# The RWKV chunk recurrence in 128x128 products, its inverse blocks joined in the batched solve

## The chip, the cores and the metric

One core of one Trainium2 chip runs the whole kernel. The metric is the device time of one execution in microseconds (us). The kernel before was run three times: 3341.92, 3346.59 and 3361.79 us, median 3346.59 us.

## The reference

One layer of a hybrid network over 512 latent tokens of width 2048 and 256 context tokens. One input projection feeds an mLSTM group and an RWKV-7 group of 16 heads (64 wide); both run forwards and backwards. An output projection and a gated convolutional FFN follow. The part that matters here is the RWKV scan, done per direction and head:

```python
def step(s, xs):
    r_t, w_t, k_t, v_t, kk_t, a_t = xs
    s = (s * w_t[:, :, None, :]
         - jnp.einsum("bhvk,bhk->bhv", s, kk_t)[..., None] * (kk_t * a_t)[:, :, None, :]
         + v_t[..., :, None] * k_t[..., None, :])
    return s, jnp.einsum("bhvk,bhk->bhv", s, r_t)
...
y_f, s_f = rwkv7_scan(..., state[2], False)
y_b, s_b = rwkv7_scan(..., state[3], True)
y = y_f + y_b
```

The latent scans start from the final state of the context scans.

## The kernel before

The dense products (input projections, output projection, FFN) hold nearly all the work of TensorE. Each takes a weight tile of 128x1024 floats that `wload` loads on SP's queue (L349) into one of 3 raw buffers (WRAW = 3); ScalarE rounds it to a high part (L299), VectorE takes the rest as a low part (L300), and TensorE makes three products of it (L370 to L372, L403 to L405 and their like).

The RWKV group works on 8 pairs of heads, two directions, and chunks of 64 tokens: 8 chunks of latent and 4 of context tokens for a pair and direction, 192 chunk steps in all. For a pair, `prep` makes the scaled keys and receivers of the chunks (KR, BK) and the products G between them, and stores these in a DRAM tile `GK_d` (L748 and L759 are two of the stores). `tsolve` inverts the 32x32 diagonal blocks of the chunks' triangular matrices for many chunks at once, one problem to a partition, on VectorE; it stores the blocks in DRAM (`ts_o`, L803, and back into `GK_d`, L808).

`chain_load` loads the operands of two chunks (`r_GK` L820 to L823, the values `r_UV` L825, an inverse block `t_XT` L830) and builds the off-diagonal block of the inverse with eight 32x32 products (L834, L838, through the PSUM tag `ct`). There are 96 such loads. `chain_step` then makes one chunk's products: the state against keys and receivers (L859, 128x128), two 64x64 products of G with the values (L861), two 64x64 products with the inverse (L865), the new state (L868, 128x128), and for latent tokens two 128x64 products for the output (L871). ScalarE copies results from PSUM to SBUF in between, VectorE updates the state `r_M`. The output is stored once for two chunks (L900), and `finalize_pair` loads it again (L921), normalises it and transposes it.

Every DMA named here is issued by SyncE (SP), on one queue, in order. The order of all instructions on every engine is fixed when the program is built, by a scheduler that runs a timeline simulation over the instructions (`schedule_with_timeline_sim=True`); weight loads are given a higher priority there (L343). So a weight load stands in SP's order somewhere between the loads and stores of the RWKV part.

Of the kernel before, what the change touches and what calls it, by code (L numbers as in the profile page):

```python
# [34 lines left out]
# column offsets inside w_in  # L35
# [4 lines left out]
# channel-major weight tiles  # L40
# [3 lines left out]
# columns of the per-channel vector pack  # L44
# [52 lines left out]
def body(tc, A, dbg=None):  # L97
# [28 lines left out]
    PB = {"acc": 2, "pre": 2, "ct": 1, "R": 3}  # L126
# [11 lines left out]
    # ---------------------------------------------------------------- constants  # L138
# [17 lines left out]
    gmask = cload("gmask", [P, 2, P])  # L156
# [11 lines left out]
    # the biases in a sigmoid, halved: sigmoid(x) = 1/2 + tanh(x / 2) / 2 shares its tables with Exp  # L168
# [6 lines left out]
    # ---------------------------------------------------------------- adaLN  # L175
# [12 lines left out]
    def ada_chunk(j, c0=0, n=512):  # L188
        """columns c0 to c0 + n of a chunk for both c"""
# [29 lines left out]
    def ada_late(j, after=None):  # L219
        """a chunk for c alone: DVE accumulates over the K tiles, the PE adds the partitions up"""  # L220
# [31 lines left out]
    def rsqrt_big(dst, src, scale, eps_ap, n):  # L252
# [3 lines left out]
        # one Newton step: y (1.5 - 0.5 x y^2)  # L256
# [45 lines left out]
    class HT:  # L302
        """hi/lo operand [128, 16 kt, n]"""
# [29 lines left out]
    # ---------------------------------------------------------------- weights  # L333
# [41 lines left out]
    def proj2(srcs, H):  # L375
        """two products side by side, for operands that are still coming in"""
# [14 lines left out]
    def proj_tm(t, H, evac):  # L391
        """token-major: [128 tok, 256 col] per token tile, two token tiles to a bank"""
# [16 lines left out]
    # ---------------------------------------------------------------- mLSTM  # L409
# [20 lines left out]
    def conv1d(pt, j, n, dst):  # L430
        """centred conv over tokens of PSUM pt -> dst"""
# [31 lines left out]
    def after_key(d, dst, lf, mi):  # L463
        """i and the decay after the key: exclusive suffix (fwd) / prefix (bwd) sums"""
# [5 lines left out]
    def to_tok(cols, srcs):  # L470
        """rows [64, 128] -> columns of tokb"""
# [19 lines left out]
    def gates_x():  # L491
        mi, lf, b2, mm = gates("x", NX)
        for d in range(2):
# [4 lines left out]
            for j in range(4):  # L498
# [9 lines left out]
                # i minus the sums, in the place of i  # L508
# [7 lines left out]
    def keep(pt, n, dst, fn=None):  # L516
        """a product's tile to DRAM"""
# [51 lines left out]
        # exponents, then the weights, in the score layout [key, query]  # L569
# [75 lines left out]
    # ---------------------------------------------------------------- RWKV  # L645
    lw = {}
    la = {}
    Mst = DT("Mst", [NPAIR, 2, P, P])
# [5 lines left out]
    def vproj(p, H, seg):  # L654
        """token-major v of two pairs, to DRAM"""
# [23 lines left out]
    def prep(p, s, seg, d=None):  # L679
        """operands of one direction's eight chunks of latent tokens, or of both directions' four of context"""  # L680
# [24 lines left out]
        BK = rp("r_BK", [P, 8, 128], 1)  # L705
# [26 lines left out]
        GK_d = DT("GK_d", [P, 2, 8, 256], 16)  # L732
        G_d = GK_d[:, 0].rearrange("p c (h t) -> p c h t", t=128)
        KB_d = GK_d[:, 1]
        sp.dma_start(KB_d[:, :, 0:kc], KR[:, :, 0:kc])
        # G^T[(b|k) s, (kappa|r) t] per chunk and head
        for hf in range(2):
            G = rp("r_Gp", [P, 4, 2, 128], GPB)
            gd = d if x else hf
            pgs = [PS("pre", [P, 4, 128]) for _ in range(2)]  # L740
            for c4 in range(4):
                for h, pg in enumerate(pgs):
                    hs = slice(64 * h, 64 * h + 64)
                    c = 4 * hf + c4
                    pe.matmul(pg[:, c4, 0:kc], BK[hs, c, :], KR[hs, c, 0:kc], start=True, stop=True)  # L745
            for h, pg in enumerate(pgs):
                dve.tensor_tensor(G[:, :, h, 0:kc], pg[:, :, 0:kc], gmask[:, gd, None, 0:kc].to_broadcast([P, 4, kc]), ALU.mult)
            sp.dma_start(G_d[:, 4 * hf:4 * hf + 4, :, 0:kc], G[:, :, :, 0:kc])  # L748
        # (b|k) e^(cum_C - cum), token-major, for the state
        for hf in range(2):  # L750
# [8 lines left out]
            sp.dma_start(KB_d[:, cs, kc:kc + 128], bt)  # L759
# [4 lines left out]
        for d in dirs:  # L764
            u = Unit()
            u.p, u.d, u.seg, u.nch, u.c0 = p, d, seg, nch, c0[d]
            u.GK_d, u.KB_d, u.G_d, u.gC, u.kd = GK_d, KB_d, G_d, gC, kd
# [3 lines left out]
    def tsolve(units):  # L771
        """(I - A^T)^-1 of the 32x32 diagonal blocks, a problem to a partition (backward: transposed)"""
# [7 lines left out]
        def blocks(u, b):  # L780
            """the unit's diagonal blocks in DRAM, and their partitions here"""
            bs = slice(32 * b, 32 * b + 32)
            q = u.p0 + b * u.q
            yield slice(q, q + u.q), u.G_d[bs, u.c0:u.c0 + u.nch, :, bs].rearrange("s c h t -> (c h) s t")

        for u in units:
            u.q, u.p0, u.so = 2 * u.nch, off[u.d], so
# [21 lines left out]

    def chain_load(u, tt):  # L810
        """operands of two chunks, and (I - A^T)^-1 put together from its blocks"""
        kc = 128 if u.seg == "x" else 64
        o = K()
        cu = u.c0 + 2 * tt
        GK = rk("r_GK", [P, 2, 2, 256], 6)
        o.G = GK[:, 0].rearrange("p c (h t) -> p c h t", t=128)
        o.KB = GK[:, 1]
        o.UV = rk("r_UV", [P, 2, 128], 6)
        if u.seg == "x":
            sp.dma_start(GK, u.GK_d[:, :, cu:cu + 2, :])  # L820
        else:
            sp.dma_start(o.G[:, :, :, 0:kc], u.G_d[:, cu:cu + 2, :, 0:kc])
            sp.dma_start(o.KB[:, :, 0:kc + 128], u.KB_d[:, cu:cu + 2, 0:kc + 128])  # L823
        po = (u.p % 2) * 128
        sp.dma_start(o.UV[64:128], v_d[u.seg][u.p // 2, tt, :, po:po + 128].rearrange("(b t) v -> t b v", b=2))  # L825
        fwd = u.d == 0
        fa, fb = (slice(0, 32), slice(32, 64)) if fwd else (slice(32, 64), slice(0, 32))
        XT = rk("t_XT", [64, 4, 32], 2)
        q = u.p0 + (0 if fwd else u.q) + 4 * tt
        sp.dma_start(XT[fa], u.so[1 if fwd else 0, q:q + 4].rearrange("a s t -> s a t"))  # L830
        pw = PS("ct", [64, 256])
        px = pw[:, 128:256]
        for i in range(4):
            pe.matmul(pw[fb, 32 * i:32 * i + 32], o.G[fa, i // 2, i % 2, fb], XT[fa, i, :], start=True, stop=True)  # L834
        ws = XT.rearrange("s a t -> s (a t)")
        act.copy(ws[fb], pw[fb, 0:128])
        for i in range(4):
# [634 lines left out]
```

## Time and profile before

| what | value |
|---|---|
| median of three runs | 3346.59 us |
| span of the profiled execution | 3344.3 us |
| PE (TensorE) busy | 3246.0 us, 97% |
| DVE (VectorE) busy | 2097.5 us, 63% |
| ACT (ScalarE) busy | 1197.9 us, 36% |
| POOL (GpSimd) busy | 51.0 us, 2% |

The page gives the profiled execution's time as its span; it agrees with the median to 2.3 us. Busy time of PE is the time during which a matmul was under way; a matmul of full-precision operands is two records in the trace. In a timeline row the first column is the start and the second the time to the end of the last instruction; matmuls overlap, so the distance from one start to the next, not the duration, is what a product costs TensorE. Rows of SPq are DMA issues on SyncE's queue; their duration is the time that the issue holds the queue, not the transfer. The RWKV part lies between about 244 and 1697 us of the span; before it is the conditioning, behind it the output projection's rest and the FFN.

### The profile page before, as it was taken

What the parts mean: (1) busy time and instruction counts of PE and PEld (TensorE: products, weight loads), DVE (VectorE), ACT (ScalarE), POOL (GpSimd) and SP (SyncE); (2) the same over time, 40 slices, a digit from 0 to 9 for tenths busy, and PEclk for the clock granted to TensorE, in tenths of its full rate; (3) what the DMA queues carried; (4) which work ended last, traced back from release to release, by engine and by line L of the source; (5) the groups of instructions that cost most, each with busy time, mean ns of one, the idle gap of its engine ahead of it and who ended that gap; (6) DMA issues with size and microseconds to landing.
All of it is one profiled execution on the core that took longest, in us unless ns stands there. A gap on an engine that the chain in (4) does not pass through costs nothing.

```text
span 3344.3 us, 50011 instructions
## 1 busy us (share of the span) xinstructions
PE 3246.0 (97%) x18566; PEld 2610.8 (78%) x18566; DVE 2097.5 (63%) x4010; ACT 1197.9 (36%) x2474; POOL 51.0 (2%) x113
## 2 busy tenths in 40 slices
PE   8999999999999999999998899999999999999998
PEld 5688778787787878777677688888888888888887
DVE  2578777777475776665754787465555555555657
ACT  4356544333334444344323432232222222222323
POOL 0000101000000000000000000000000000000000
PEclk9999999999999999999999999999999999999999
DMA  8878656566567678776764355333333333333332
GB/s 280 306 241 243 185 156 161 162 212 206 187 188 230 194 234 253 207 233 214 260 211 130 99 190 183 95 95 97 96 97 95 95 100 96 95 95 95 101 95 101
DMA packets 391938, 552.97 MB, mean 165 GB/s; under 512 B 131312, under 2 KB 256520, under 8 KB 391440
## 3 DMA queue, kind: packets, MB, share of 16 engines
q1 hardware_dynamic: 382048, 536.41, 51.9%
q10 hardware_dynamic: 9648, 13.37, 1.1%
q8 instruction: 147, 2.41, 0.3%
q14 instruction: 95, 0.78, 0.1%
HBM read 459.06 MB, written 90.61 MB: 164 GB/s over the span
## 4 chain that ended last, share of the span: by engine, by line
PE 82%; DMA 8%; DVE 6%; ACT 2%; issue 1%; SPq 1%; DVEq 0%; ACTq 0%
PE acc L372 12%; PE acc L371 12%; PE acc L370 12%; PE acc L1350 5%; PE acc L1351 5%; PE acc L1352 5%; DMA am<-in_wmod 3%; PE R L859 2%; PE R L861 2%; PE R L865 2%; PE pre L195 2%; PE acc L405 2%; PE acc L404 2%; PE pre L745 2%; PE acc L403 2%
## 5 line engine op out<-in xcount | busy, mean ns | idle before, releaser
L299 ACT CAST whi<-wraw 128x512 fp32r<-128x512 f32 (+1 forms) x948 | 569.7, 604 | 1319.8 <-PE acc L371 715.9
L300 DVE TENSOR_TENSOR wlo<-wraw,whi 128x512 fp32r<-128x512 f32 (+1 forms) x948 | 629.2, 666 | 457.5 <-ACT whi L299 440.6
L370 PE MATMUL acc<-H,whi 128*128 128x512 f32 x1920 | 761.7, 397 | 4.0 <-ACT ev L520 3.0
L372 PE MATMUL acc<-H,wlo 128*128 128x512 f32 x1920 | 761.4, 397 | 3.7 <-DVE wlo L300 3.7
L371 PE MATMUL acc<-H,whi 128*128 128x512 f32 x1920 | 761.1, 396 | 0.0
L372 PEld LDWEIGHTS acc<-H,wlo 128*128 128x128 f32 x1920 | 362.7, 189 | 83.8 <-DVE wlo L300 4.9
L370 PEld LDWEIGHTS acc<-H,whi 128*128 128x128 f32 x1920 | 362.9, 189 | 82.8 <-ACT ev L520 3.2
L371 PEld LDWEIGHTS acc<-H,whi 128*128 128x128 f32 x1920 | 362.8, 189 | 79.2 <-issue 3.6
L1354 DVE SCALAR_TENSOR_TENSOR x<-acc,mod,x 128x512 f32<-128x512 f32 (+1 forms) x192 | 135.6, 706 | 221.9 <-PE acc L1352 221.8
L1298 DVE SCALAR_TENSOR_TENSOR f_cv<-upad,fvec,f_cv 128x512 f32<-128x512 f32 x352 | 263.7, 749 | 7.2
L1350 PE MATMUL acc<-fh,whi 128*128 128x512 f32 x640 | 253.2, 396 | 0.0
L1351 PE MATMUL acc<-fl,whi 128*128 128x512 f32 x640 | 253.1, 396 | 0.0
L1352 PE MATMUL acc<-fh,wlo 128*128 128x512 f32 x640 | 253.1, 396 | 0.0
L232 DVE SCALAR_TENSOR_TENSOR adacc<-am,csil,adacc 128x512 f32<-128x512 f32 x240 | 179.4, 748 | 91.8 <-DMA am<-in_wmod 89.8
L404 PE MATMUL acc<-whi,H 128*128 128x256 f32 x512 | 155.7, 304 | 0.0
L403 PE MATMUL acc<-whi,H 128*128 128x256 f32 x512 | 154.6, 302 | 0.3 <-DVE ev L434 0.3
L405 PE MATMUL acc<-wlo,H 128*128 128x256 f32 x512 | 152.7, 299 | 0.3 <-DVE wlo L300 0.3
L1352 PEld LDWEIGHTS acc<-fh,wlo 128*128 128x128 f32 x640 | 120.2, 188 | 29.1
L1350 PEld LDWEIGHTS acc<-fh,whi 128*128 128x128 f32 x640 | 120.2, 188 | 29.0
L1351 PEld LDWEIGHTS acc<-fl,whi 128*128 128x128 f32 x640 | 120.2, 188 | 29.0
L876 DVE SCALAR_TENSOR_TENSOR r_M<-r_M,r_gC,R 64x64 f32<-64x64 f32 x352 | 98.3, 279 | 48.1 <-ACT r_yt L872 33.0
L1236 PE MATMUL acc<-H,whi 128*128 128x512 f32 x256 | 101.6, 401 | 9.0 <-ACT H L299 7.9
(346 smaller groups left out, 4837.3 us busy)
## 6 DMA issues: line engine op xcount, KB each, us to landing
am<-in_wmod SPq DMA_DIRECT2D x128, 512.0 KB
wraw<-in_wup SPq DMA_DIRECT2D x88, 512.0 KB
wraw<-in_wgate SPq DMA_DIRECT2D x88, 512.0 KB
wraw<-in_wdn SPq DMA_DIRECT2D x88, 512.0 KB
wraw<-in_wcm SPq DMA_DIRECT2D x72, 512.0 KB
r_GK<-GK_d SPq DMA_DIRECT2D x64, 512.0 KB
wraw<-in_wtm SPq DMA_DIRECT2D x56, 512.0 KB
GK_d<-r_Gp SPq DMA_DIRECT2D x32, 512.0 KB
```

What stands on the lines that cost most here:

```text
L299: act.copy(hi, t)
L300: dve.tensor_tensor(lo, t, hi.bitcast(F32), ALU.subtract)
L370: pe.matmul(pt[:, :n], hi(k8), H.h(k), start=k == 0, stop=False)
L371: pe.matmul(pt[:, :n], hi(k8), H.l(k), start=False, stop=False)
L372: pe.matmul(pt[:, :n], lo(k8), H.h(k), start=False, stop=k == KT - 1)
L403: pe.matmul(o, H.h(k)[:, xs], hi(k4), start=first, stop=False, skip_group_check=True)
L404: pe.matmul(o, H.l(k)[:, xs], hi(k4), start=False, stop=False, skip_group_check=True)
L405: pe.matmul(o, H.h(k)[:, xs], lo(k4), start=False, stop=k == KT - 1, skip_group_check=True)
L1298: dve.scalar_tensor_tensor(cv, u[:, a:a + GH, b:b + GW], fvec[:, f, tap:tap + 1], cv, ALU.mult, ALU.add)
L1350: pe.matmul(pt, hi(m)[:, k, :], th[:, cs], start=k == 0, stop=False)
L1351: pe.matmul(pt, hi(m)[:, k, :], tl[:, cs], start=False, stop=False)
L1352: pe.matmul(pt, lo(m)[:, k, :], th[:, cs], start=False, stop=k == GF - 1)
```

## The change

- `prep` stores stacked operands for each chunk in a DRAM tile `AB_d` [128, 8, 4, kc] and the triangular matrices in `T_d` [128, 8, 64]. Where it stored KR, G and the transposed BK in 1 + 2 + 2 DMAs for a unit of eight chunks, it now issues 3 + 12 + 6 (latent) or 2 + 8 + 6 (context).
- `tsolve` also joins the inverse blocks: for groups of two chunks, 128x128 block-diagonal operands N and W (zeroed on POOL, filled by DMA and by ScalarE copies), one product of 128x32 with N (L854) and one with W (L859) for each group; the result is copied to SBUF and stored back in `T_d` (L864). The eight 32x32 products in `chain_load` are gone, with the PSUM tag `ct`.
- `chain_v` loads state and values stacked: `r_UV` is [128, 2, 2, 2, 64], filled by four DMAs of 64 partitions (L881), each value block twice. It has 8 buffers.
- `chain_load` loads `r_GK` in one DMA (L890), and the inverse into the two diagonal halves of `r_T` (a memset on POOL and two DMAs, L894).
- `chain_step` makes three kinds of product, all 128x128 on TensorE: A (two for latent, one for context; L908 and L910), T (one; L917), B (two or one). The new state is written by VectorE straight into the next chunk's `r_UV`; the output is the sum of A's and B's halves (a VectorE addition per half), stored by two DMAs (L980).
- The PSUM tag `R` has 4 buffers instead of 3; `dynamic_dma_scratch_size=1024` is passed to the builder; comments are removed.

Over the program the products on TensorE (two records each) change by -2160 and +1024: 192 + 512 + 128 + 192 new ones are L854 and L859, L908, L910, L917. SP issues 3042 DMAs instead of 1754.

```diff
@@ prep
-        GK_d = DT("GK_d", [P, 2, 8, 256], 16)
...
-        sp.dma_start(KB_d[:, :, 0:kc], KR[:, :, 0:kc])
+        AB_d = DT("AB_d" if x else "ABc_d", [P, 8, 4, kc], 16 if x else 8)
+        T_d = DT("T_d", [P, 8, 64], 24)
...
+        sp.dma_start(AB_d[LO, :, 0, :], KR[LO, :, 0:kc])
+        if x:
+            for o, i in ((LO, HI), (HI, LO)):
+                sp.dma_start(AB_d[HI, :, 1, o], KR[HI, :, i])
...
-            sp.dma_start(G_d[:, 4 * hf:4 * hf + 4, :, 0:kc], G[:, :, :, 0:kc])
...
+            sp.dma_start(AB_d[HI, cs, 0, :], G[HI, :, 0, 0:kc])
+            sp.dma_start(AB_d[LO, cs, 1, :], G[LO, :, 1, 0:kc])
+            sp.dma_start(T_d[LO, cs, :], G[LO, :, 0, 0:64])
+            sp.dma_start(T_d[HI, cs, :], G[HI, :, 1, kc - 64:kc])
+            if x:
+                sp.dma_start(AB_d[:, cs, 2, HI], G[:, :, 0, HI])
+                sp.dma_start(AB_d[:, cs, 3, LO], G[:, :, 1, LO])
...
-            sp.dma_start(KB_d[:, cs, kc:kc + 128], bt)
+            sp.dma_start(AB_d[:, cs, 2, 0:64], bt[:, :, LO])
+            sp.dma_start(AB_d[HI, cs, 3, kc - 64:kc], bt[LO, :, HI])
+            sp.dma_start(AB_d[LO, cs, 3, kc - 64:kc], bt[HI, :, HI])
@@ tsolve
+        for k in range(0, len(units), 2):
...
+            pool.memset(N, 0.0)
+            pool.memset(W, 0.0)
...
+                        sp.dma_start(dst[64 * h:64 * h + 64, u.gs, :], src)
+                for i in range(4):
+                    sp.dma_start(N[32 * i:32 * i + 32, u.gs, 32 * i:32 * i + 32], beside(u, i))
...
+            for g in range(ng):
+                pe.matmul(pw[:, g, :], N[:, g, :], XT[:, g, :], start=True, stop=True)
+            for i in range(4):
+                r = slice(32 * i, 32 * i + 32)
+                act.copy(W[r, :, r], pw[r])
+            for g in range(ng):
+                pe.matmul(px[:, g, :], W[:, g, :], XB[:, g, :], start=True, stop=True)
+            O = rp("t_XT", [P, 8, 32], 1)[:, 0:ng]
+            dve.tensor_copy(O, px)
+            for u in us:
+                for i in range(4):
+                    sp.dma_start(beside(u, i), O[32 * i:32 * i + 32, u.gs, :])
@@ chain_v, chain_load
+    def chain_v(u, tt):
+        t = rk("r_UV", [P, 2, 2, 2, 64], 8)
+        po = (u.p % 2) * 128
+        for h in range(2):
+            v = v_d[u.seg][u.p // 2, tt, :, po + 64 * h:po + 64 * h + 64].rearrange("(b t) v -> t b v", b=2)
+            for k in range(2):
+                sp.dma_start(t[LOHI[1 - h], :, k, h, :], v)
+        return t
...
-        for i in range(4):
-            pe.matmul(pw[fb, 32 * i:32 * i + 32], o.G[fa, i // 2, i % 2, fb], XT[fa, i, :], start=True, stop=True)
...
+        o.AB = rk("r_GK", [P, 2, 4, kc], 6)
+        sp.dma_start(o.AB, u.AB_d[:, cu:cu + 2])
+        o.T = rk("r_T", [P, 2, 128], 6)
+        pool.memset(o.T, 0.0)
+        for hs in LOHI:
+            sp.dma_start(o.T[hs, :, hs], u.T_d[hs, cu:cu + 2, :])
@@ chain_step
-        pe.matmul(pR[0:kc], o.KB[:, ci, 0:kc], u.M, start=True, stop=False, skip_group_check=True)
-        for h, hs in enumerate(H2):
-            pe.matmul(pR[0:64, hs], o.G[64:128, ci, h, 0:64], UV[64:128, hs], start=False, stop=True, skip_group_check=True)
...
+        both(pA, o.AB[:, ci, 0:2], MV)
+        Rs = rk("r_Rs", [P, 64], 4)
+        for h, hs in enumerate(LOHI):
+            act.copy(Rs[hs], pA[hs, h])
+        pe.matmul(pU, o.T[:, ci, :], Rs, **f)
+        for h, hs in enumerate(LOHI):
+            act.copy(UV[hs, h], pU[hs])
+        both(pB, o.AB[:, ci, 2:4], UV)
...
+                    for h in range(2):
+                        sp.dma_start(u.y_d[at(u, i), :, 64 * h:64 * h + 64].rearrange("(b t) v -> t b v", b=2), o.y[LOHI[1 - h]])
```

SP's order, near the end of the RWKV part, where the first weight tiles of the output projection (`in_wout`) are loaded. Before:

```order
L228 DMA am_16687<-in_wmod 128x1024
L349 DMA wraw_17160<-in_wout 128x1024
L642 DMA hm_d_128<-r_r_16131 128x512
L1227 DMA ev_16763<-hm_d_128 128x512
L1227 DMA ev_16767<-hm_d_128 128x512
...
L593 DMA H_16861<-rows_d_130 128x256
L587 DMA H_16859<-rows_d_130 128x128
L593 DMA H_16859<-rows_d_130 128x128
L587 DMA H_16861<-rows_d_130 128x128
L575 DMA H_16862<-rows_d_130 128x512
L587 DMA H_16861<-rows_d_130 128x128
L349 DMA wraw_17199<-in_wout 128x1024
```

And in the change, the same place:

```order
L349 DMA wraw_18071<-in_wout 128x1024
L349 DMA wraw_18160<-in_wout 128x1024
L851 DMA t_X_12546<-T_d_12033 32x4x32 x4
...
L864 DMA T_d_10549<-t_XT_12536 128x1x32 x4
...
L894 DMA r_T_12893<-T_d_10549 64x2x64 x2
...
L881 DMA r_UV_13137<-v_x_136 64x2x64 x3
...
L980 DMA yr_d_12890<-r_yt_13529 64x2x64 x2
...
L565 DMA H_17860<-vc_d_115 128x2x256
L568 DMA H_17860<-in_nmask 128x256
L349 DMA wraw_18199<-in_wout 128x1024
```

Between two weight loads there were 28 DMAs; now there are 605 (412 rows of the order, many of them for several DMAs). Over the whole program before, no two neighbouring weight loads have more than 29 DMAs between them. In the change five stretches have more than 100, in their order 111, 121, 262, 254 and 605 DMAs (1353 in all; they follow weight loads 126, 140, 161, 180 and 190 of 482); the next longest has 68.

PE's order at the same place. Before, the small products stand between dense ones:

```order
L404 MATMUL acc_15514<-whi_15691,H_2688 128x256
L405 MATMUL acc_15514<-wlo_15692,H_2687 128x256
L865 MATMUL R_12415<-r_Rs_12419,r_GK_12289 64x64
L868 MATMUL R_12400<-r_UV_12273,r_GK_12272 128x128
L871 MATMUL R_12400<-r_UV_12273,r_GK_12272 64x64 x2
L865 MATMUL R_12415<-r_Rs_12419,r_GK_12289 64x64
L838 MATMUL ct_12457<-r_GK_12451,t_XT_12455 32x32 x4
L859 MATMUL R_12503<-r_M_2457_11995,r_GK_12434 128x128
L861 MATMUL R_12503<-r_UV_12435,r_GK_12434 64x64 x2
L403 MATMUL acc_15513<-whi_15695,H_2687 128x256
L404 MATMUL acc_15513<-whi_15695,H_2688 128x256
```

In the change there is a stretch of 300 rows with no dense product of a loaded weight, from this

```order
L370 MATMUL acc_17607<-H_2687,whi_17648 128x512
L371 MATMUL acc_17607<-H_2688,whi_17648 128x512
L372 MATMUL acc_17607<-H_2687,wlo_17649 128x512
L854 MATMUL pre_12514<-t_XT_12494,t_X_12492 128x32 x8
L859 MATMUL pre_12515<-t_XB_12495,t_Y_12493 128x32 x8
L854 MATMUL pre_12568<-t_XT_12548,t_X_12546 128x32 x8
L917 MATMUL R_12939<-r_Rs_12942,r_T_12893 128x64
...
L908 MATMUL R_14953<-r_UV_14663,r_GK_14833 128x64 x2
...
L640 MATMUL pre_16358<-c_ident_90,r_kd_16172 128x128
L1316 MATMUL acc_17915<-H_17759,whi_17918 128x512
```

where the last row is the next dense product (L1316, the output projection). Of the products in between, 376 are those of the chain and the join (248 of L908, 64 of L917, 64 of the join), 144 are other products of up to 128 columns, and 52 go over 257 or 512 columns. The other four stretches look alike and are shorter.

## Rows read from the trace of the kernel before

**Rows 1.** page parts 1 and 4: span; busy time by engine; chain by engine

```profile
span 3344.3 us, 50011 instructions
...
PE 3246.0 (97%) x18566; PEld 2610.8 (78%) x18566; DVE 2097.5 (63%) x4010; ACT 1197.9 (36%) x2474; POOL 51.0 (2%) x113
...
PE 82%; DMA 8%; DVE 6%; ACT 2%; issue 1%; SPq 1%; DVEq 0%; ACTq 0%
```

**Rows 2.** windows view, RWKV stretch: busy us of each engine, clock, DMA share, GB/s

```profile
244.00:1697.00 1453.00, 1410.01 (x9858) 1125.92 (x9857) 1000.72 (x2244) 611.40 (x1457) 48.15 (x90) 0.97 0.69 207
```

**Rows 3.** lines view, PE: the chain's products

```profile
L859 PE MATMUL R<-r_M,r_GK 128*128 128x128 f32 (+1 forms) x384 | 87.9, 311 | 3.4 <-DMA r_GK<-GK_d 2.2 <-DVE r_M L876 1.0
...
L865 PE MATMUL R<-r_Rs,r_GK 64*64 64x64 f32 x768 | 84.5, 232 | 2.8 <-DVE r_GK L839 2.4 <-ACT r_Rs L863 0.3
L868 PE MATMUL R<-r_UV,r_GK 128*128 128x128 f32 x352 | 76.9, 302 | 0.0
...
L871 PE MATMUL R<-r_UV,r_GK 128*64 128x64 f32 x512 | 58.5, 239 | 2.3 <-ACT r_UV L866 2.3
...
L834 PE MATMUL ct<-t_XT,r_GK 32*32 32x32 f32 x768 | 42.8, 194 | 1.0 <-DMA t_XT<-ts_o 0.9
```

**Rows 4.** timeline of PE about 1001 to 1009 us: start, time, engine, line, operation

```profile
1001.00 0.49 PE L859 MATMUL R<-r_M,r_GK 128*128 128x128 f32 x2
1001.42 0.44 PE L861 MATMUL R<-r_UV,r_GK 64*64 64x64 f32 x4
...
1004.91 0.43 PE L838 MATMUL ct<-r_GK,t_XT 32*32 32x32 f32 x8
1005.28 0.44 PE L865 MATMUL R<-r_Rs,r_GK 64*64 64x64 f32 x4
1005.65 0.39 PE L404 MATMUL acc<-whi,H 128*128 128x256 f32 x1
1005.87 0.28 PE L405 MATMUL acc<-wlo,H 128*128 128x256 f32 x1
...
1007.63 0.38 PE L859 MATMUL R<-r_M,r_GK 128*128 128x128 f32 x2
1007.85 0.39 PE L868 MATMUL R<-r_UV,r_GK 128*128 128x128 f32 x2
1008.17 0.45 PE L871 MATMUL R<-r_UV,r_GK 128*64 128x64 f32 x4
1008.54 0.44 PE L861 MATMUL R<-r_UV,r_GK 64*64 64x64 f32 x4
```

**Rows 5.** timeline of PE: first and last of 351 groups of products

```profile
306.96 0.28 PE L964 MATMUL acc<-whi,H 128*128 128x256 f32 x1
307.08 0.28 PE L965 MATMUL acc<-wlo,H 128*128 128x256 f32 x1
307.29 0.43 PE L859 MATMUL R<-r_M,r_GK 128*64 128x128 f32 x2
...
1616.57 0.44 PE L865 MATMUL R<-r_Rs,r_GK 64*64 64x64 f32 x4 [0.32 <-ACT r_Rs L863]
```

**Rows 6.** source views, SP issues: count, min/median/max ns, first and last start

```profile
L825 SPq DMA_DIRECT2D r_UV<-v_x x64: 579/611/1178, 698.8 to 1567.8; - x64
...
L900 SPq DMA_DIRECT2D yr_d<-r_yt x64: 319/544/1368, 880.0 to 1621.2; - x64
...
L349 SPq DMA_DIRECT2D wraw<-in_wup x88: 327/328/328, 1838.1 to 3201.2; - x88
...
L349 SPq DMA_DIRECT2D wraw<-in_wdn x88: 327/328/328, 2053.0 to 3281.4; - x88
```

**Rows 7.** timeline of SP: first, second, last of 35 issues in a dense stretch

```profile
469.01 0.49 SPq L803 DMA_DIRECT2D ts_o<-t_X  x1
469.55 0.48 SPq L808 DMA_DIRECT2D GK_d<-t_X  x1
...
490.43 0.63 SPq L823 DMA_DIRECT2D r_GK<-GK_d  x1
```

More of the change, by code (lines that the diff above doesn't have):

```diff
@@ new lines, in beside @@
+    def beside(u, i):
+        r = 64 * (i // 2) + u.fa
+        c = u.c0 + i % 2
+        return u.T_d[r:r + 32, c:c + u.nch - 1:2, u.fb:u.fb + 32]
+    LOHI = (slice(0, 64), slice(64, 128))
+    def chain_v(u, tt):
+        t = rk("r_UV", [P, 2, 2, 2, 64], 8)
+        po = (u.p % 2) * 128
+        for h in range(2):
+            v = v_d[u.seg][u.p // 2, tt, :, po + 64 * h:po + 64 * h + 64].rearrange("(b t) v -> t b v", b=2)
+            for k in range(2):
+                sp.dma_start(t[LOHI[1 - h], :, k, h, :], v)
+        return t
@@ L824, in chain_load @@
[L824 to L832, printed above, removed]
@@ L842, in chain_init @@
[L842 to L850 removed]
+        kc = 128 if u.seg == "x" else 64
+        o.AB = rk("r_GK", [P, 2, 4, kc], 6)
[4 more added lines that the diff above has]
+            sp.dma_start(o.T[hs, :, hs], u.T_d[hs, cu:cu + 2, :])
@@ L875, in chain_step, with both @@
-        for hs in H2:
-            dve.scalar_tensor_tensor(u.M[hs, hs], u.M[hs, hs], u.gC[hs, u.c0 + c:u.c0 + c + 1], pM[hs, hs], ALU.mult, ALU.add)
-        if last:
-            sp.dma_start(Mst[u.p, u.d], u.M)
+        MV, UV = o.V[:, ci, 0], o.V[:, ci, 1]
+        bank = PS("R", [P, 5, 64])
+        f = dict(start=True, stop=True, skip_group_check=True)
+        def both(out, w, rhs):
+            if x:
+                for h in range(2):
+                    pe.matmul(out[:, h, :], w[:, h, :], rhs[:, h, :], **f)
+            else:
+                pe.matmul(out.rearrange("p h v -> p (h v)"), w.rearrange("p h t -> p (h t)"), rhs.rearrange("p h v -> p (h v)"), **f)
@@ new lines, in chain_step @@
+        pA, pU, pB = bank[:, 0:2], bank[:, 2], bank[:, 3:5]
+        both(pA, o.AB[:, ci, 0:2], MV)
[6 more added lines that the diff above has]
+        both(pB, o.AB[:, ci, 2:4], UV)
+        if x:
+            for h in range(2):
+                hs = LOHI[1 - h]
+                act.copy(o.y[hs, ci, :], pA[hs, h])
@@ L880, in chain @@
+        if nxt is not None:
+            for h, hs in enumerate(LOHI):
+                dve.scalar_tensor_tensor(nxt(h), MV[hs, h], u.gC[hs, u.c0 + c:u.c0 + c + 1], pB[hs, h], ALU.mult, ALU.add)
+        if x:
+            for h in range(2):
+                hs = LOHI[1 - h]
+                dve.tensor_tensor(o.y[hs, ci, :], pB[hs, h], o.y[hs, ci, :], ALU.add)
     def chain(us, mid):
+        x = us[0].seg == "x"
+        n = us[0].nch // 2
+        at = lambda u, i: i if u.d == 0 else n - 1 - i
@@ L882, in chain @@
+        nV = []
         for u in us:
-            chain_init(u)
-        n = us[0].nch // 2
+            V = chain_v(u, at(u, 0))
+            nV.append(V)
+            for h, hs in enumerate(LOHI):
+                m = V[hs, 0 if u.d == 0 else 1, 0, h]
+                if x:
+                    sp.dma_start(m, Mst[u.p, u.d, hs])
+                else:
+                    pool.memset(m, 0.0)
+            if x:
+                u.y_d = DT("yr_d", [4, P, 128], 16)
         for i in range(n):
-            if us[0].seg == "x" and i == 1:
+            if x and i == 1:
@@ L902, in chain @@
+            if x:
+                for u, o in zip(us, ops):
+                    for h in range(2):
+                        sp.dma_start(u.y_d[at(u, i), :, 64 * h:64 * h + 64].rearrange("(b t) v -> t b v", b=2), o.y[LOHI[1 - h]])
+        if x:
             mid()
@@ L1440, in pack @@
     o["selg"] = (idx[:, None] % 32 == np.arange(2)[None]).astype(f)
-    gm = np.zeros((P, 2, P), f)
+    gm = np.zeros((P, 2, 2, P), f)
     s_ = (idx % 64)[:, None]
     t_ = (idx % 64)[None]
-    strict = idx[None] < 64
-    gm[:, 0] = np.where(strict, s_ < t_, s_ <= t_)
-    gm[:, 1] = np.where(strict, s_ > t_, s_ >= t_)
+    for h in range(2):
+        strict = (idx[None] // 64) == h
+        half = np.where(((idx[:, None] // 64) != h) & ~strict, f(0.5), f(1))
+        gm[:, 0, h] = np.where(strict, s_ < t_, s_ <= t_) * half
+        gm[:, 1, h] = np.where(strict, s_ > t_, s_ >= t_) * half
     o["gmask"] = gm
```

131 lines of the change are left out of this document (61 added, 70 removed).

## Prediction

> **What bounds the kernel now.** I read the page first: PE is busy for 3246.0 us of the 3344.3 us span, and 82% of the chain that ended last is PE's own work [rows 1]. The windows view of the RWKV stretch says the same there: PE is busy for 1410 of 1453 us, while DVE has 450 us free, ACT 840 us, POOL nearly all, and the DMA engines are busy for 0.69 of the time at 207 GB/s [rows 2]. So the sum of PE's slots sets the time, and whatever lies on another engine is hidden, as long as the next weight tile is there when PE asks for it. The views that follow are PE's lines and its timeline, for what the chain's products cost; then SP's issues by line and its timeline, because the order shown above moves SP more than anything else.
>
> **PE: what is removed.** The lines view gives counts in records, two to a product [rows 3]; the slots come from the timeline, from one start to the next [rows 4].
> - L859, a 128x128 product ahead of two 64x64 ones: 1001.42 - 1001.00 = 0.42 us, 192 times: 81 us.
> - L865, two 64x64: 1005.65 - 1005.28 = 0.37 us, 192 times: 71 us; its twin L861 the same: 71 us.
> - L834, four 32x32, and its twin L838 (1005.28 - 1004.91 = 0.37 us): 96 times each: 71 us.
> - L868: 1008.17 - 1007.85 = 0.32 us, 176 times: 56 us. L871: 1008.54 - 1008.17 = 0.37 us, 128 times: 47 us.
>
> That is 397 us. They stand in 351 groups between dense products, and going into one costs PE something as well: L965 ahead of such a group takes 307.29 - 307.08 = 0.21 us where the same product before it takes 0.12 [rows 5], and the first dense product behind a group takes 1005.87 - 1005.65 = 0.22 us [rows 4]. With 0.09 and 0.10 us that is 0.19 x 351 = 67 us (first group at 307.29, last at 1616.57). In all 464 us.
>
> **PE: what is added.** 1024 products of the 128x128 kind. L859 at 1007.63, with L868 of the same shape behind it, has a slot of 0.22 us [rows 4]; the 0.42 at 1001.00 holds the step to the 64x64 tile behind it. Nothing changes shape any more, so I take 0.22: 225 us. The upper end is 0.42, a rival below. PE's path becomes 3344.3 - 464 + 225 = **3105 us**, if nothing else stops PE.
>
> **DVE, ACT and POOL.** 256 more additions on DVE, 504 more copies on ACT and 144 more memsets on POOL stand beside hundreds of free us on each [rows 2]; I cost them at nothing. If that cover were gone they would show as waits of L908 or L917. The DMA engines carry some 18 MB more; at 207 GB/s for a share of 0.69 that is 60 us of engine time against 0.31 x 1453 = 450 us free, nothing too.
>
> **SP: what the change does to the queue.** SP gets 1288 more DMAs. This isn't spread evenly. Before, a weight load has at most 29 other DMAs between it and the next. In the new order there are five stretches without a weight load, of 111, 121, 262, 254 and 605 DMAs, 1353 in all. The queue is in order: the next dense tile can't start to load until all of them are issued. In these stretches PE's order holds only small work, and behind it dense products that wait for the tile.
>
> *What the 1353 issues take.* 464 of them load 64 partitions in pieces; the row of that kind is the old r_UV load, median 0.611 us. 327 store 64 partitions; the nearest row is L900, 0.544 us. The other 562 I take at the price of a plain weight load, 0.328 us [rows 6]. This sums to 646 us. Between issues lies 469.55 - 469.01 - 0.49 = 0.05 us [rows 7], 68 us more: 714 us, or 0.53 each. The other view is the densest stretch of the old queue, much of it the same kind of loads and stores of pieces: 35 issues from 469.01 to the last one's end at 491.06, or 0.63 each [rows 7], which would be 852 us. I take the middle, 0.58: **785 us**. The ends far apart are 0.328 for each issue without a gap (444 us) and 0.63 (852 us); 0.58 is nearer the second because nearly three in five of these issues are of the dear kinds.
>
> *What PE has to do meanwhile.* In the longest stretch 376 products of 0.22 us (83 us), and 144 small and 52 wider ones, which I estimate at 42 us by their columns: 125 us. The other four, counted alike, give 15, 16, 35 and 34 us: 225 us together. And three weight tiles may be there ahead, one for each raw buffer. The FFN's loads give the price of a tile: 264 of them (the up, gate and down rows, 88 each) lie between 1838.1 and 3281.4 us [rows 6], 5.5 us of PE each, so up to 16 us a stretch, 81 us in all. Cover: 306 us.
>
> *Exposed:* 785 - 306 = 479 us, in which PE stands still although it would have dense work. Waits for semaphores on SP come on top; I cost them at nothing here, and as a rival below.
>
> **The sum.** 3105 + 479 = 3584 us against the profiled execution, whose span is 2 us under the median of 3346.59: **3586 us**, 7% slower. At 0.53 us an issue it is 3518, at 0.63 us 3653; this case's own range, with 30 us for the cover, is 3490 to 3690. The saving of 239 us is undone where the five stretches expose as much: (306 + 239) / 1353 = 0.403 us an issue is the point that decides.
>
> **A rule to weigh.** The rows of one kind of issue range from 0.328 to 0.611 us [rows 6], so the price follows what is moved. [...]
>
> **The rivals.**
> - *Faster: SP keeps up.* If pieces of 64 partitions cost the queue no more than a plain load when nothing else crowds the DMA engines, all issues go at 0.328 us, without a gap or with one of 0.05: 444 to 511 us, 138 to 205 exposed, 3245 to 3312 us. It decides below 0.403 us an issue. For it: L900 has been issued in 0.319 us at its best, and the rows of before were taken while the DMA engines were busy for 0.69 of the time. Against it: the old r_UV load never took less than 0.579 us in 64 issues [rows 6]. Chance 0.16.
> - *No change.* A mean issue between 0.38 and 0.43 us balances the saving: 3313 to 3380 us. It needs no more than that the dear kinds cost 0.46 instead of 0.544 to 0.611 us at 0.328 for the rest [rows 6]; against it the medians by themselves give 0.48. Chance 0.11. [...]
> - *Slower still: the queue stops.* SP's stretches hold stores of results that the chain has yet to make (T_d from L864, yr_d from L980) and loads into buffers that it has yet to free. A store that waits at the head of the queue holds the loads behind it, which the chain needs next; PE's small work would then follow the issues instead of lying beside them. If all 225 us of it loses its place: 3811 us; half, 3700. For it: work and queue depend on each other in every chunk. Against it: 8 buffers of r_UV and 6 of r_GK and r_T let loads run ahead. Chance 0.14.
> - *The products stay dear.* If a 128x128 product keeps a slot of 0.42 us, the new ones cost 430 us and the saving is 34; outside of the stretches, where SP hides them, at most 205 us come on top: up to 3791 us. The slot at 1007.63 speaks against it. Chance 0.04.
>
> **How the numbers follow.** My forecast has 0.55: 3586 us. A difference under 1% (33 us) can't be told from no change here. The range, 3300 to 3790 us, takes in the forecast's own, no change, the upper end of the faster case and most of the third and fourth; it leaves out some 0.13 below and 0.06 above. Faster by over 1%: 0.16; within 1%: 0.11; slower: 0.73.
>
> **What would show it.** In the new profile PE idles in five stretches, ended by a weight tile (wraw, through L299 or L300), the longest by far at the start of the output projection, where L1316's first product waits for some 200 us; SP's timeline there shows issues with hardly a gap between them. The lines view gives L908 and L917 slots of 0.22 us and no product with 32 or 64 rows in the chain; behind the RWKV part the rows are as before. I am wrong if PE stays busy through these stretches (SP faster than 0.40 us an issue, or the tiles there earlier than the order says), or if PE's idle time is ended by r_T, r_UV or yr_d instead, which is the third rival.

## The result: 17% slower, and 350 us beyond the forecast

The change takes 3935.75 us (median of 4 runs, 3934.54 to 3936.90) against 3351.36 us for the kernel before in the same comparison: a ratio of 1.174, 95% interval 1.171 to 1.177. The sign was forecast (3586 us); the size lies outside the range of 3300 to 3790 us.

The page of the change, its span, its busy times, PE's share by slice, and the engines of the chain that ended last:

```profile
span 3935.1 us, 48383 instructions
...
PE 3293.6 (84%) x16294; PEld 2722.0 (69%) x16294; DVE 2130.6 (54%) x4186; ACT 1318.0 (33%) x2989; POOL 98.6 (3%) x257
...
PE   8997999676975984674375589999999999999998
...
PEclk9999999686975975655567799999999999999999
...
PE 60%; DMA 15%; SPq 10%; DVE 7%; ACT 4%; issue 3%; POOL 0%; DVEq 0%; ACTq 0%; POOLq 0%
```

PE has 2272 matmul records fewer than before [rows 1] and yet is busy 48 us longer, while the granted clock falls in the slices where PE idles (to 5 tenths in the twentieth, where PE is busy for 3 tenths). With each 2 us of busy time counted at the clock granted in it, PE is busy for 3017 us against 3199 before, 182 us less. DMAs and SP's queue, 9% of the chain of before [rows 1], now hold 25% of it. Windows of the change (us of each engine, granted clock, DMA share, GB/s): 200 us out of the longest stretch without a weight load, and the dense end.

```profile
1700.00:1900.00 200.00, 91.03 (x396) 78.02 (x394) 107.95 (x262) 59.90 (x186) 8.66 (x19) 0.53 0.64 174
2300.00:3800.00 1500.00, 1478.41 (x6452) 1207.75 (x6452) 876.65 (x1312) 438.39 (x712) 0.00 (x0) 0.99 0.34 112
```

No engine and not the DMA engines (0.64, before 0.69 [rows 2]) are full in the first of them. The prices of the new issues on SP (count, min/median/max ns, first and last start):

```profile
L881 SPq DMA_DIRECT2D r_UV<-v_x x256: 573/605/1686, 889.7 to 2010.0; - x128
...
L894 SPq DMA_DIRECT2D r_T<-T_d x192: 573/602/1710, 461.9 to 2026.3; - x192
...
L980 SPq DMA_DIRECT2D yr_d<-r_yt x128: 574/580/1615, 1097.0 to 2047.5; - x128
```

They are as dear as the nearest rows of before said [rows 6]: 0.58 to 0.605 us at the median. Added up over the five stretches without a weight load, the 1353 issues hold the queue for 775 us, 0.573 each. But the stretches last 1033 us: 67, 85, 187, 184 and 508 us from the end of one weight load's issue to the next (the last from 1636 to 2145). What PE waits for longest in this profile (us, times, longest):

```profile
PE pre L854 <- DMA t_X<-T_d: 110.4, 13, 50.5
PE pre L773 <- DVE r_Gp L758: 46.3, 16, 5.9
PE R L908 <- issue: 41.5, 6, 10.0
PE pre L854 <- DMA t_XT<-ts_o: 40.1, 6, 12.3
PE acc L1316 <- ACT H L299: 37.6, 7, 15.3
PE R L908 <- DMA r_GK<-AB_d: 34.9, 16, 9.5
...
PE acc L370 <- ACT whi L299: 14.4, 5, 9.6
```

A weight tile (a wait for `whi` or `wlo`) is far from the head of the list. The waits that it ended add up to 31 us of 627; those ahead of the chain's products (L908, L910, L917) make 180 us, of the join's (L854, L859) 159 and of prep's 87. The output projection (L1316) waits for H, its other operand, which is made from the results of the heads. In the longest stretch its first product started at 2063 us, 82 us before the next weight tile was issued:

```profile
2063.01 1.22 PE L1316 MATMUL acc<-H,whi 128*128 128x512 f32 x2 [15.26 <-ACT H L299]
```

Of SP's own waits over the whole program, the longest behind the weight loads' wait for a free buffer, and one of the chain's:

```profile
SPq L228 <- DVE adacc L232: 76.2, 57, 3.0
SPq L228 <- DMA am<-in_wmod: 74.5, 36, 6.0
...
SPq L980 <- DVE r_yt L931: 27.3, 29, 5.3
```

L228 loads the weights of the conditioning, which have nothing to do with the chain; L980 stores the chain's output. The longest single wait of PE stands at the join: its product with N waits for blocks that went through DRAM. One solve and join in SP's timeline and then in PE's, both of the change:

```profile
1896.30 3.33 SPq L829 DMA_DIRECT2D T_d<-t_X  x4
1899.68 2.32 SPq L829 DMA_DIRECT2D T_d<-t_Y  x4
1902.04 1.29 SPq L849 DMA_DIRECT2D t_XT<-ts_o  x2
1903.37 1.27 SPq L849 DMA_DIRECT2D t_XB<-ts_o  x2
1904.74 2.50 SPq L851 DMA_DIRECT2D t_X<-T_d  x4
1907.28 1.27 SPq L849 DMA_DIRECT2D t_XT<-ts_o  x2
1908.59 1.28 SPq L849 DMA_DIRECT2D t_XB<-ts_o  x2
1909.91 2.54 SPq L851 DMA_DIRECT2D t_X<-T_d  x4
```

```profile
1914.05 1.89 PE L854 MATMUL pre<-t_XT,t_X 128*128 128x32 f32 x8 [3.36 <-DMA t_X<-T_d]
1917.68 3.59 PE L859 MATMUL pre<-t_XB,t_Y 128*128 128x32 f32 x16 [1.74 <-POOL t_X L837]
1933.33 3.59 PE L854 MATMUL pre<-t_XT,t_X 128*128 128x32 f32 x16 [12.06 <-DMA t_XT<-ts_o]
1936.75 0.66 PE L917 MATMUL R<-r_Rs,r_T 128*128 128x64 f32 x2
1938.10 0.66 PE L917 MATMUL R<-r_Rs,r_T 128*128 128x64 f32 x2 [0.69 <-DMA r_T<-T_d]
```

Stores (L829), loads that read them (L851), the products with N (L854), copies into W, the products with W (L859), stores of the result (L864); then the same for the next two units. Each waits for the one before, each DMA stands in one queue at 0.6 us, and the T products of the chain (L917) wait for the blocks that the join stores. From 1794 to 1936 us no chunk step gets its T product. From the first output store of one group of 32 latent steps (two pairs of heads, both directions) to that of the third after it, it is 880 to 1475 us before (L900), 198 us a group, and 1097 to 1953 us now (L980), 285 us a group.

### The profile page after: what moved, and what is told of

It is laid out like the page before. It is cut to its first block, busy times and chain, and to the rows that moved or that the text cites. A ratio compares the mean times of both kernels' runs of the same rounds, so it can differ in the third digit from the quotient of the medians.

```text
span 3935.1 us, 48383 instructions
## 1 busy us (share of the span) xinstructions
PE 3293.6 (84%) x16294; PEld 2722.0 (69%) x16294; DVE 2130.6 (54%) x4186; ACT 1318.0 (33%) x2989; POOL 98.6 (3%) x257
## 2 busy tenths in 40 slices
DMA packets 582535, 571.43 MB, mean 145 GB/s; under 512 B 379248, under 2 KB 455176, under 8 KB 582032
## 4 chain that ended last, share of the span: by engine, by line
PE 60%; DMA 15%; SPq 10%; DVE 7%; ACT 4%; issue 3%; POOL 0%; DVEq 0%; ACTq 0%; POOLq 0%
PE acc L370 10%; PE acc L372 10%; PE acc L371 9%; PE acc L1430 4%; PE acc L1432 4%; PE acc L1431 4%; DMA am<-in_wmod 4%; PE R L908 2%; SPq L829 2%; PE pre L195 1%; DVE adacc L232 1%; DMA r_GK<-AB_d 1%; PE acc L1316 1%; PE acc L1317 1%; PE acc L1318 1%
## 5 line engine op out<-in xcount | busy, mean ns | idle before, releaser
L908 PE MATMUL R<-r_UV,r_GK 128*128 128x64 f32 x1024 | 209.4, 369 | 131.0 <-issue 41.5
L908 PEld LDWEIGHTS R<-r_UV,r_GK 128*128 128x128 f32 x1024 | 196.6, 280 | 161.4 <-issue 63.1
L854 PE MATMUL pre<-t_XT,t_X 128*128 128x32 f32 x192 | 37.1, 343 | 152.2 <-DMA t_X<-T_d 110.4
L405 PE MATMUL acc<-wlo,H 128*128 128x256 f32 x512 | 152.5, 301 | 4.9 <-DVE wlo L300 4.9
L404 PE MATMUL acc<-whi,H 128*128 128x256 f32 x512 | 153.4, 300 | 0.0
L1316 PE MATMUL acc<-H,whi 128*128 128x512 f32 x256 | 104.1, 412 | 55.9 <-ACT H L299 37.6
L927 DVE SCALAR_TENSOR_TENSOR r_UV<-r_UV,r_gC,R 64x64 f32<-64x64 f32 x320 | 89.0, 278 | 109.4 <-ACT r_yt L924 84.3
```

Of the source, the lines that this page charges most:

```text
L404: pe.matmul(o, H.l(k)[:, xs], hi(k4), start=False, stop=False, skip_group_check=True)
L908: pe.matmul(out[:, h, :], w[:, h, :], rhs[:, h, :], **f)
```

## The experiments

All ratios are to the kernel before, run on the same chip (medians 3348 to 3351 us). The expectations name their theories by letters. Q: SP's in-order queue sets the time once it is full. P: each issue costs the same, full queue or not. S: the number of SP's issues sets the time, whatever they are for. J: the path through solve and join, where each step waits for the one before. C: the new chain waits for its own results, or PE's clock falls. K: the fallen clock makes the stretch long.

**More issues, old products.** In the kernel before, `chain_load` got 13, in another run 6, loads that nobody reads:

```diff
+        for i in range(13):        # the other run: 6
+            sp.dma_start(rk("dmy", [P, 2, 128], 2)[64:128], v_d[...].rearrange("(b t) v -> t b v", b=2))
```

> The kernel before with 13 more loads in every chain_load (1248 loads of 64 partitions from v_d into a scratch tile that nobody reads), so SP issues 3002 DMAs as the change does, and PE's products are those of before. Theory Q (SP's in-order queue, some 0.6 us for each issue, sets the time): its order has stretches of 172 and 633 DMAs without a weight load; 805 x 0.65 = 523 us less about 300 us of PE work and tiles at hand, so 3450 to 3700 us. Rival C (the change is slow because the new chain waits for its own results or because PE's clock falls): no such chain here, 3340 to 3390 us.

> As the run with 13 more loads, but 6 in every chain_load: 576 more issues, 2330 in all on SP. Its order has one stretch without a weight load, of 122 DMAs, and by the last tile of the input projections 160 of 192 chunk steps are placed (the kernel before: 166; the one with 13 loads: 128). Theory Q (SP's queue decides once it is full, and the chain then falls behind the dense work and is left standing alone at the end): SP has room for these, 3345 to 3450 us. Rival P (each issue costs the same, full queue or not; 636 us for 1248): 3630 to 3660 us.

Measured: 3987.56 us (1.191, 1.188 to 1.194) and 3519.75 us (1.050, 1.046 to 1.054). So 576 loads cost 169 us, 0.29 each, and the next 672 cost 468, 0.70 each. Added loads on SP alone can make the kernel before slower than the change is, with none of the new products. The price of one added issue, in SP's rows of the run with 13, and what SP waits for ahead of these issues:

```profile
L827 SPq DMA_DIRECT2D dmy<-v_x x832: 573/577/2397, 1020.5 to 2411.6; - x167
```

```profile
SPq L827 <- DMA dmy<-v_x: 322.7, 404, 3.7
SPq L827 <- DMA dmy<-v_c: 137.9, 177, 4.0
```

The added loads share two scratch buffers, and SP stands still until a buffer's last load has landed: 461 us in this run, 256 us in the one with 6. So the two prices hold the waits for these buffers as well as the issues; a queue that fills up would give the same picture, but these runs don't show it by itself.

Both runs came out above the upper end that the theory of a full queue (Q) gave them; the same price for each added load whatever the queue holds (P, 3630 to 3660 us for the run with 6) is refuted by the low price of the first 576.

**Other queues.** The change with DMAs moved from SP (`sp.dma_start` becomes `act.dma_start` or `pool.dma_start`): prep's stores and the join to ScalarE and the chain's loads to GpSimd; all of these to GpSimd; prep's stores and the join to ScalarE alone (there with the lead of the weight loads lowered to 300 as well).

> The change with the DMAs of prep's AB_d and T_d stores and of the join issued by ScalarE, and the loads of chain_v and chain_load issued by GpSimd; SP is back at 1522 DMAs, the products are the same. Theory Q: PE's path of 3105 us plus what the one stretch left (360 DMAs, some 75 us exposed) costs: 3150 to 3300 us. Rival C (chain's own waits, PE's clock): the chain and its order are nearly the same, so 3700 to 3940 us. If ScalarE's or GpSimd's issues hold up the chain: between, 3300 to 3600 us.

> The change with all of these DMAs (prep's AB_d and T_d stores, the join, chain_v and chain_load) issued by GpSimd, 1520 there and 1522 on SP. Theory Q: as long as GpSimd issues one in under 0.8 us, 3150 to 3300 us; at 1 us or more its own queue becomes the bound, 3400 us or above. Rival C: 3700 to 3940 us.

> The change with prep's AB_d and T_d stores and the join's DMAs issued by ScalarE (848 of them), the chain's loads staying on SP (2194 issues), and the lead of the weight loads lowered to 300. Theory S: 2194 issues, fewer than the 2330 that cost the kernel before 169 us: 3250 to 3500 us. Theory J: 3650 to 3800 us.

Measured: 3826.68 us (1.143, 1.140 to 1.145), 4167.77 us (1.244, 1.241 to 1.247) and 3854.42 us (1.150, 1.148 to 1.152). Halving SP's issues gave back 109 us, where theory Q gave 636 or more. An issue costs ScalarE and GpSimd what it costs SP, as one row each of the first and the second run shows (SP's medians for the two lines are 0.575 and 0.605 us), and the path through the join is as long as it was: PE's longest wait in the first run is still the same one.

```profile
L864 ACTq DMA_DIRECT2D T_d<-t_XT x128: 309/582/1467, 426.5 to 1852.0; - x128
```

```profile
L881 POOL DMA_DIRECT2D r_UV<-v_x x256: 585/599/644, 1025.8 to 2279.8; - x128
```

```profile
PE pre L854 <- DMA t_X<-T_d: 105.5, 9, 43.3
```

So occupation of SP's queue alone is not the cause: theories Q and S failed in all three, and J, with 3650 to 3800 us for the last, came nearest, though still under it; rival C's 3700 to 3940 us holds for the first run and not for the second.

**Another order.** Only the scheduler's lead of the weight loads: `AHEAD_X = 3000` becomes 12000, or 2000.

> The change with the scheduler's lead of the weight loads raised from 3000 to 12000: the stretches of 111 to 262 DMAs go, and the last one grows from 605 to 1187. Theory Q: the same number of issues, but the cover is less at the end: 1187 x 0.62 = 736 us against some 250 us of PE work in it, and what was exposed before is saved; 3600 to 3900 us. Rival C: no change, 3900 to 3950 us.

> The change with the scheduler's lead of the weight loads lowered from 3000 to 2000: the same 3042 issues on SP, but by the last tile of the input projections 160 steps are placed instead of 107, the last stretch without a weight load has 97 DMAs instead of 605, and three others have some 255. Theory Q: less chain work stands alone, 3500 to 3750 us. Rival S: the same number of issues, 3900 to 3940 us.

Measured: 3924.53 us (1.172, 1.169 to 1.175) and 3860.55 us (1.153, 1.148 to 1.157). Theory Q missed both, and S the second; the first is what rival C gave. Where the weight loads stand among the issues is worth 75 us at best. With 767 instead of 1353 DMAs in long stretches the kernel is still 15% slower, so the picture of five bad stretches is too narrow: the whole part is slow.

**The clock.** Four more products in every latent step, into an unused part of its PSUM bank:

```diff
+            for _ in range(2):     # behind the products with A, and again behind those with B
+                pe.matmul(bank[:, 5:8, :], o.AB[:, ci, 0, :], <192 columns of o.AB>, **f)
```

> The change with four more 128x128 products over 192 columns in every latent chunk step, into an unused part of the step's PSUM bank, so that PE idles less in the stretch where its granted clock fell to 0.53. Rival K (the fallen clock is what makes the stretch long): the clock stays higher and the time falls by 50 us or more, below 3890 us. Theory Q: the products stand in PE's idle time or on top, 3920 to 4080 us.

Measured: 3906.71 us (1.165, 1.161 to 1.170), with the clock up from 0.53 to 0.64 in the same window:

```profile
1700.00:1900.00 200.00, 95.28 (x525) 86.40 (x524) 94.72 (x234) 52.70 (x167) 7.88 (x19) 0.64 0.59 159
```

Some 29 us less although PE has more to do; both K and Q missed it. The fallen clock costs something: in the change six products of L908 take 0.21 us each at a granted clock of 1.00 (1406.95 to 1408.21 us) and 0.43 at 0.50 (1444.12 to 1446.68). The run raised it only in part, so what a full clock would give back is not shown; nearly all of the loss stayed.

**Parts taken away.** Without the join in `tsolve`; without the chain's loads (r_GK and r_T are constants, r_UV gets a memset); without both; and without prep's stores into AB_d as well. And without the join, but with 384 other loads in its place that no one waits for.

```diff
-        for k in range(0, len(units), 2):   # the join, down to the stores of O
...
-        sp.dma_start(o.AB, u.AB_d[:, cu:cu + 2])
+        o.AB = still[u.seg]
...
-            sp.dma_start(AB_d[...], ...)    # the last of the four
...
+                    D = rk("dmy", [P, 4, 64], 2)    # 12 for a unit: 4 of 64, 8 of 32 partitions
+                    sp.dma_start(D[...], A["ident"][...])
```

> The change without the join of the inverse blocks in tsolve (its loads, memsets, products, copies and stores are left out; r_T then holds blocks that were not joined): 384 fewer issues on SP, 2658 in all. By the last tile of the input projections 154 steps are placed instead of 107. Theory Q: 3400 to 3600 us. Rival S (it is the price of each issue on SP alone): 384 x 0.62 = 238 us less, 3690 us. Rival C (the new chain steps are themselves slow): 3850 us or above.

> The change without the loads of chain_load and chain_v: r_GK and r_T are constant tiles, r_UV is filled by a memset on GpSimd; prep's stores, the solve and the join stay, and the chain's products, copies and stores too. SP issues 2370 DMAs. Theory S (the number of issues on SP): 672 fewer than the change; like the kernel before with 2330 (3520 us), less the products' saving of 239: 3300 to 3500 us. Theory J (the solve with the join is a path of its own, of loads, stores and products that wait for each other, and sets the pace of the jobs): about as slow as with the queues split, 3700 to 3850 us.

> As the run without the chain's loads, and without the join in tsolve as well: 1986 issues on SP. This leaves PE's path of the change: 3105 us less 42 us for the join's 192 products is 3063. Theory S: 3070 to 3200 us. Theory J: the same, since the join is gone. If the new products are dearer than 0.22 us each, or their steps too long, 3250 us or more: then the step on PE's saving was wrong as well.

> As the run without the chain's loads and without the join, and prep's stores into AB_d left out as well (nobody reads them there): 1618 issues on SP, fewer than the kernel before has; PE has the change's products but the join's. Theory S: what was left above PE's path of 3063 us (3366 - 3063 = 303) was SP's, and 368 issues fewer give 3070 to 3200 us. If 3300 us or more, the saving on PE isn't there or is lost at another place, such as the four mLSTM heads and the finalisation at the end.

> The change without the join, with as many other loads on SP in its place (384, of constants into a scratch tile that nobody reads, 128 of 64 partitions and 256 of 32): 3042 issues again, none of them in the path from solve to chain. Theory J (the join's loads, products and stores wait for each other and for the solve, and the chain behind waits for them): 3580 to 3700 us, as without the join (3605). Theory S (SP's issues, whatever they are for): 384 x 0.5 to 0.65 us more than without the join, 3800 to 3940 us.

| kernel | SP issues | us | ratio (95%) |
|---|---|---|---|
| the change | 3042 | 3935.75 | 1.174 (1.171 to 1.177) |
| without the join, other loads instead | 3042 | 3843.24 | 1.147 (1.146 to 1.149) |
| without the join | 2658 | 3605.06 | 1.076 (1.072 to 1.079) |
| without the chain's loads | 2370 | 3730.33 | 1.114 (1.112 to 1.116) |
| without both | 1986 | 3365.82 | 1.005 (1.003 to 1.007) |
| and without AB_d's stores | 1618 | 3301.46 | 0.985 (0.982 to 0.987) |

The join costs 331 us (3936 - 3605), or 364 where the chain doesn't load (3730 - 3366); the chain's loads 206 or 239. Together that is 570 of the 585 us by which the change is slower; the join's 192 products (42 us at 0.22) go with it. Without the chain's loads alone it went as J said (3700 to 3850 us), and S missed by 230 us. The run with other loads splits the join: 238 us for 384 issues that nobody waits for (3843 - 3605), 0.62 each, and 93 us for what the join waits for (3936 - 3843). The split is not clean. SP waits for 65 us there (43 and 22 at the two lines) for the two scratch buffers of the other loads, so 238 us is too much for the issues alone and 93 too little for the join. And the order differs: that run's stretches without a weight load are of 116, 534 and 604 DMAs. It went as theory S said and not as J did; but S fails on the queues and J on this one, so both are parts of one thing.

The theory of the full queue gave the run without the join 3400 to 3600 us, nearly met; S gave the two runs without both 3070 to 3200 us (J gave the first the same), missed by 166 us and by 101. The last run has PE's products of the change without the join's, and fewer issues on SP than the kernel before. Its page's line on PE and its timeline, around a group of chain products (L869, ten records; L404 and L405 dense):

```profile
PE 3039.5 (92%) x15910; PEld 2508.8 (76%) x15910; DVE 2103.8 (64%) x4170; ACT 1276.2 (39%) x2914; POOL 115.9 (4%) x228
```

```profile
901.75 1.33 PE L869 MATMUL R<-r_UV,still_x 128*128 128x64 f32 x10
902.88 0.36 PE L404 MATMUL acc<-whi,H 128*128 128x256 f32 x1
903.09 0.28 PE L405 MATMUL acc<-wlo,H 128*128 128x256 f32 x1
903.20 0.55 PE L869 MATMUL R<-r_UV,still_x 128*128 128x64 f32 x4
```

A product has the slot that was forecast: 902.88 - 901.75 = 1.13 us for five. But the dense product behind the group takes 0.21 us, nearly as before [rows 4]: the step on the way out is still paid. The one ahead of the next group takes 903.20 - 903.09 = 0.11 us, where it took 0.21 before [rows 5]: the step on the way in is gone. Over that run the medians are 0.20 us behind a group and 0.12 ahead of one, for dense products of 256 columns. In its longest stretch without a weight load (119 DMAs, 1368 to 1523 us) PE is busy for half of the time, and loads of the conditioning weights (L228) are 43% of the chain that ended last there: this part has nothing to do with the join or the chain's loads.

**Fewer loads.** The second copy of each value block made on GpSimd:

```diff
-            for k in range(2):
-                sp.dma_start(t[LOHI[1 - h], :, k, h, :], v)
+            sp.dma_start(t[LOHI[1 - h], :, 0, h, :], v)
+            pool.tensor_copy(t[LOHI[1 - h], :, 1, h, :], t[LOHI[1 - h], :, 0, h, :])
```

> The change with the second copy of each value block in r_UV made by a GpSimd copy instead of a load: 192 fewer issues on SP (2850). The order keeps a stretch of 839 DMAs without a weight load at the end. Theory S: 192 x 0.63 = 121 us less, 3800 to 3830 us. Theory J: the join's path is as long as before, 3900 to 3950 us.

Measured: 3838.12 us (1.145, 1.143 to 1.147), 98 us less for 192 issues, 0.51 each, somewhat less than S gave and far from J's none. S was nearer than J, with 0.63 for each. None of the versions that compute everything comes within 14% of the kernel before.

## Why the prediction was right in sign and wrong in size

- **The cause named, an in-order queue with too many issues: right, as far as it goes.** 576 and 1248 idle loads slowed the old kernel by 169 and 636 us, and 384 off any path cost 0.62 us each, all with the waits for their scratch buffers in it. But halving SP's issues gave back 109 us only.
- **The price of an issue: 0.58 forecast, 0.62 measured** (775 / 1353 = 0.573, and the gap of 0.05 [rows 7]). Over 1353 issues that is 843 us with the gaps, 58 us more than the 785. The saturated stretch of before (0.63) was the better of the two views.
- **What PE stands still for, with the waits costed at nothing: the step that failed most.** The prediction has PE's small work lying beside the issues and PE waiting for the next weight tile. Of PE's 627 us of waits, weight tiles ended 31; 426 stand ahead of products of the chain, the join and prep, and 232 of these were ended by the landing of the chain's or the join's own loads (t_X, t_XT, r_GK, r_UV, r_T). Ahead of the longest stretch four tiles of the output projection had been issued by 1636 us, and its first product waited for H. The third rival had this mechanism: small work that follows the issues, with the waits on SP on top. I gave it 0.14 and at most 3811 us, and placed the waits at the chain's buffers. The stretches last 1033 us, where issues and gaps make 843; the other 190 us are waits of SP that the sum has at nothing. The largest part of them, 70 us, is loads of the conditioning weights (L228), which no rival names; the chain's output stores (L980) make 23 us and the join's DMAs (L849, L851, L864) 16.
- **PE's saving: 239 us forecast, some 197 there.** PE is busy for 3246.0 us before [rows 1] and 3039.5 us in the last run of the table: 206.5 us less, of which the join's 192 products at 0.22 us take back 42. But the granted clock fell in that run too; counted at the granted clock, as above, the busy time is 239 us less (3199 and 2960), 197 with the join's products. The other 42 us lie in the 67 for going in and out of 351 groups, booked as saved ("nothing changes shape any more"). Only 258 of these groups had a dense product directly ahead of them and 218 one directly behind, which makes 45 us by the prediction's prices; and in the last run the way out was still paid, 0.085 us for 244 groups, 21 us. The way in was saved.
- **Together** 58 + 190 + 42 = 290 of 350 us on the sum's own terms; the rest is not accounted for. This keeps the cover of 306 us as it was forecast, which no run confirms: PE was busy for 633 us of the five stretches, at a granted clock of 0.58 to 0.72. So how the 350 us divide is worked out, not shown by a run. Read from PE's page instead, 64 us of them are idle time and 287 busy time: 479 us more idle and 239 less busy were forecast, and 543 more idle and 48 more busy came. That the idle time came out so near is luck, since PE idled for other things than was said.
- **The signs that were named:** the longest stretch stands where it was said, ahead of the output projection, and is 508 us long. The idle time in it ends with t_X, t_XT, r_T and r_GK rather than with a weight tile: that was the sign of the third rival. And L1316 waited for H, 38 us in all, and not for a weight tile for some 200 us. The slot of a chain product is 0.22 us only where the clock is at its upper level (1.00); at the lower one (0.50) it is 0.43, which is also the median of the change.
- **The price of an issue, by what is moved.** The runs show 0.33 us for a whole weight tile of the FFN and 0.57 to 0.61 us for pieces of 64 partitions at the median, and both 0.30 and 0.57 us (least and median) for one and the same line, L851; there is no one price.
- **What stays open:** how much of the time with the split queues (3827 and 3854 us) is ScalarE's and GpSimd's issuing, and how much the landing of the DMAs; no run shortened the path itself with all its work kept. How much the full queue costs without waits for buffers is open as well, and so is the size of the packets: those under 512 B rose from 131312 to 379248, and no run changed that alone.

## What to carry to other kernels

Before operands are restacked so that the matmuls get larger, count the DMAs that the stacking takes and multiply by the price of their own form from the trace; here 1288 issues of 0.57 to 0.6 us stood against some 200 us of PE. The first added loads cost less than the later ones (0.29 and 0.70 us each, waits for their buffers included), so compare the sum with the room left in the queue, for the whole stage and not for a few bad stretches. Look also at what else waits in the same queue: a load that waits for its buffer holds all that stand behind it, 70 us of such waits in the five stretches here. And a step that sends its operands through DRAM twice in a row (stores, loads, a product, stores, loads) is a path with a length of its own: here another queue gave back 109 of 585 us.

## What the runs showed of the hardware

- An issue of 64-partition pieces held SP, ScalarE and GpSimd for 0.58 to 0.63 us at the median (SP 0.605, GpSimd 0.599, ScalarE 0.60 and 0.63), one of a 128x1024 tile SP for 0.328 us in the FFN and for 0.376 and 0.422 us in the input projections. For one and the same line the engines hardly differ: 0.605 us on SP and 0.599 on GpSimd (L881), 0.590 on SP and 0.597 on ScalarE (L759).
- In the last run of the table and in the change, the first dense product of 256 columns behind a group of the chain's full-precision ones takes 0.20 us instead of 0.12 at the median, though both use the whole 128x128 array; the one ahead of such a group takes 0.12.
- The granted clock was 0.53 over 200 us in which PE was busy for 91 us, and 0.99 where it was busy for 1478 of 1500. Of 1968 windows of 2 us over the change's span, 1406 show it at 1.00, 493 at 0.50 and 69 in between.
